# GpSimd makes the lower part of every second block of U, and U's two parts get three buffers each

## The chip, the cores and the metric

The kernel runs on one core of one Trainium2 chip. The metric is the device time of one execution in microseconds (us); lower is better. The engines that matter here are TensorE (PE, with its weight loads as PEld), VectorE (DVE), ScalarE (ACT), GpSimd (POOL), and SyncE (SP), which only issues transfers.

## The reference

The program is a two-layer network over 256 context tokens and 512 latent tokens of width 1024. Each layer has four token mixers and then a feed-forward part with product keys (PEER). Only the PEER part matters for this change. It is, cut to what is computed:

```
q = (xb @ wq).reshape(T, 8, 2, 128)
s = einsum('thcq,hckq->thck', q, keys)             # 128 keys in each of two halves of a head
sv, si = top_k(s, 16)                              # the 16 best of each half
top_s, top_j = top_k(sv[..., 0, :, None] + sv[..., 1, None, :], 16)   # of the 16 x 16 pairs
eidx = the 16 chosen experts of 128 * 128 for every token and head
gate = softmax(top_s)
act = gelu(einsum('td,thkd->thk', xb, U[eidx]))
out = einsum('thk,thkd->td', gate * act, V[eidx])
```

U and V are tables of 16384 rows of 1024 numbers per layer, all float32.

## The kernel before

**Two ways to the experts.** The last tokens of a layer (256 in layer 0, 128 in layer 1) gather just the rows of U and V that they chose. All other tokens (512 in layer 0, 384 in layer 1) are multiplied with all of U and V, in 128 blocks of 128 experts each, and a sparse array of gates decides what counts.

**A block of U.** `s_part(j, up)` (L1451 to L1463) makes one block. SyncE loads 128 x 1024 numbers into `ur`. `split` (L249 to L251) makes two parts of type float32r for TensorE: ScalarE writes the upper part `uh` (a cast, L250), and VectorE writes the lower part `ul = ur - uh` (L251). Then 24 matmuls (L254: eight slices of the width times three products of parts) sum in PSUM under the name `d.S`, ScalarE applies the gelu (`d.pa`, L247) and its queue stores the result to DRAM (`mrg.Ad`, L1472). `uh` and `ul` have two buffers each, so block j + 2 can be cast only when TensorE is done with block j. There are 128 blocks per layer, so 256 casts, 256 subtractions and 6144 matmuls.

**What stands beside it.** `s_ahead(n)` (L1468) lays out the next n blocks of U between pieces of the routing: the scores `rt.q` and `rt.k`, the searches for the best (L1556 to L1583), and `build`, which makes the gate array from one-hot rows (`rt.o`, `rt.og`, `ro.x` on VectorE, `rt.k` on TensorE, `rt.gst` on ScalarE). In layer 1 the last 62 blocks come after all routing (`trailing`).

**The gathers.** `choose(n, after)` (L1511) first uses the rows that came in two calls earlier (`use`: a multiply with sum, L1500, or an addition scaled by a weight, L244, both on VectorE), then copies the numbers of the next rows to `at` (L1522, VectorE) and has GpSimd issue one indirect DMA for each (L1527, into `grow`, of which there are 4 buffers in layer 0 and 6 in layer 1). In layer 0 each block of U carries a call for 2 rows; in layer 1 each of the last 62 blocks carries a call for 1. With `tc.issue_after` the VectorE instructions of a call stand behind the instruction `last[0]`, which is the subtraction of the block just laid out. GpSimd has no other work in these stretches.

**Order.** A scheduler orders each engine's instructions when the program is built, by its own estimate of the times. On the chip each engine runs its list strictly in that order.

After U come the 128 blocks of V (`rt.O`, `d.O`), then the next layer.

Of the kernel before, what the change touches and what calls it, by code (L numbers as in the profile page):

```python
# [13 lines left out]
A = mybir.AluOpType  # L14
# [6 lines left out]
EPS = 1e-6  # L21
# [5 lines left out]
# ---------------------------------------------------------------- layout on the host  # L27
# [90 lines left out]
def consts():  # L118
    o = {}
    for n, L in (("l", SEQ), ("c", CTX)):  # L120
        # Half of the times and of the frequencies: e and o below are the sums and differences of the tokens t and
        # their mirror images, of which the even and the odd frequencies need one each for cosine and sine.
        # 0: the filters, t against L - t; 1, 2: tokens, t + 1/2 against L - t - 1/2, and back.
# [91 lines left out]
# ---------------------------------------------------------------- the program  # L215

def body(tc, I, out, dbg=None, stop=None):
# [56 lines left out]
    def segs(n):  # L274
        """columns in PSUM banks: the latents' 512, then the context's 256 before them"""
        return [(max(0, n - 512), n)] + ([(0, n - 512)] if n > 512 else [])

    with pool("keep") as kp, pool("scr", space=DRAM) as dp:
        # ---------------------------------------------------------- persistent
# [13 lines left out]
        def inv_sqrt(o, i, scale, eps_ap_or_val):  # L293
            """(i * scale + eps) ** -0.5"""
            act(o, i, AF.Ln, scale, eps_ap_or_val)
            act(o, o, AF.Exp, -0.5)
# [10 lines left out]
        # ---------------------------------------------------------- modulation vectors  # L307
        def ada(l, rounds, wp, pp, cs, dma, bufs):
            """columns 2048 * r on; the two vectors' products lie on partitions 32 * q and 32 * q + 1"""
# [23 lines left out]
        # ---------------------------------------------------------- Hyena's filters  # L333
        def dft_part(p, n, L, kind, f):
            """two parts each of the cosines and sines of 128 frequencies"""
            t = T(p, [128, 2, 2, L // 2], F32R, "dft", 2)
            G.dma_start(t, I["dft_" + n][:, kind, f])
            if kind < 2:
                t = t.rearrange("p a b (j m) -> p a b j m", m=128)
            return (t[:, 0, 0], t[:, 0, 1]), (t[:, 1, 0], t[:, 1, 1])  # L340

        def sin_(p, t, ps, frq, bias, L):
            """sin(frq * (ps + bias)) with the argument brought to [-pi, pi]"""
# [13 lines left out]
        def spectrum(l, n, L, p, pp, dst_):  # L357
# [12 lines left out]
            # the first half of the times on the upper partitions; the second, mirrored and with the middle in the  # L370
            # place of time L, on the lower ones
# [10 lines left out]
            # forward plus and minus backward, each the sum (0) and difference (1) of a time and its mirror image  # L382
# [34 lines left out]
            # 1 / (L * (sum of the absolute values + EPS)); 1/L = 2/N is the weight of a frequency in the inverse  # L417
# [5 lines left out]
            for f in range(NC):  # L423
# [15 lines left out]
                if f == 0:  # L439
                    # the highest frequency, in the place of the sine of frequency 0  # L440
# [16 lines left out]
        # ---------------------------------------------------------- prologue  # L457
# [18 lines left out]
        # ---------------------------------------------------------- shared pieces  # L476
        def rms_scale(p, pp, srcs, n, tag, tags=(("sq", 2), ("rstd", 1))):
            """1 / sqrt(mean of squares over all rows + EPS), on every partition"""
# [14 lines left out]
        def norm_mod(hps, p, pp, x, l, which, t0, tag, cut=None):  # L493
            """what the products read, in two parts; for the tokens before and from cut on in a pool each"""
# [16 lines left out]
        def projector(wp, pp, src, tag, off=0, ks=range(8), eng=None):  # L511
            """rows of a product with h for the tokens from t0 on, by segments; early(c) fetches a row's weights"""
# [26 lines left out]
        def padded(p, zd, c, tag, bufs, t0):  # L539
            """a row block of z with two zeros before and one behind each stream, in three stretches of 256 tokens"""  # L540
# [12 lines left out]
        def conv(o, xp, taps, bias, t0):  # L553
            """o = sum of w * (token + shift) + bias; the first tap carries the bias"""
# [26 lines left out]
        # ---------------------------------------------------------- RG-LRU  # L581
# [68 lines left out]
        # ---------------------------------------------------------- RWKV-7  # L650
# [5 lines left out]
        def rwkv_prep(l, zd, t0, pp, p):  # L656
            """what the recurrences read, for both tiles of channels; the long parts go through DRAM"""
# [25 lines left out]
            for c in range(2):  # L683
# [6 lines left out]
                # -- decays, keys and the like, channels on partitions  # L690
# [72 lines left out]
                # -- the masked products N whose (1 - N)^-1 each chunk needs; the inverses of their diagonal blocks  # L763
                # of 16, row by row, with a block on each partition
# [27 lines left out]
                # the gate g: what the read-out multiplies by and adds  # L792
# [26 lines left out]
        def rwkv_load(l, st, p):  # L819
            """what all chunks read"""  # L820
# [15 lines left out]
        def rwkv_chain(l, c, t0, stt_, y, p, pp, qp):  # L836
            """the chunks of 128 tokens of one tile of channels, both directions side by side, as generators that can be
            laid out alternately: the inverses of a chunk, and its recurrence"""
# [10 lines left out]
            def inverse(step):  # L849
# [7 lines left out]
                # Wm[d, s]: C against A and R, B against A and R, with the tokens' order as a mask  # L857
# [11 lines left out]
                # XZ[g, d]: the inverse of direction d where g != d, its transpose where g == d  # L869
# [91 lines left out]
        def rwkv_out(l, t0, n, stt_, y, p, pp, tag):  # L961
            """the read-out of the chunks n of both tiles, normed as a group"""
# [34 lines left out]
        def alternate(*gens):  # L997
            """lays the generators' pieces out in turn; (n, g) begins n rounds later"""
# [6 lines left out]
        # ---------------------------------------------------------- mLSTM  # L1005
        def colmajor(ap, t0):
            """the latents' columns of a token row, walked (row, col) where they lie (col, row)"""
# [185 lines left out]
        # ---------------------------------------------------------- Hyena  # L1193
        def mix_hyena(l, n, zd, ydst, p, pp):
# [16 lines left out]
            for o in range(2):  # L1211
                # sums (0) and differences (1) of the tokens and their mirror images
# [13 lines left out]
                for f in range(NC):  # L1226
# [9 lines left out]
                    # the sine part of the transform is -q[:, 1]  # L1236
# [12 lines left out]
                # what the tokens and their mirror images have in common (0), and half their difference (1)  # L1249
# [22 lines left out]
        # ---------------------------------------------------------- the four mixers  # L1272
# [6 lines left out]
        def mixers(l, xin):  # L1279
            """xin: (pool, tile) of the residual stream"""  # L1280
# [134 lines left out]
        # ---------------------------------------------------------- PEER  # L1415
        def peer(l, xin):
# [5 lines left out]
            # the last tokens gather the rows that they chose; the others' products go over all rows  # L1422
# [21 lines left out]
            # x waits in DRAM while the routing uses its place  # L1444
# [6 lines left out]
            def s_part(j, up):  # L1451
                ur = T(up, [128, 8, 128], F32, "ur", URB[l])
                SP.dma_start(ur, I["U"][l, j])
                uh = T(up, [128, 8, 128], F32R, "uh", 2)
                ul = T(up, [128, 8, 128], F32R, "ul", 2)
                last[0] = split(ur, uh, ul)
# [10 lines left out]
            def s_ahead(n):  # L1467
                """U's products, which don't wait for the routing"""  # L1468
# [9 lines left out]
            def token_rows(t):  # L1478
                """h of a tile of tokens, a token on each partition"""
# [12 lines left out]
            # the last tokens' experts, tile by tile: row e of U, later of V for every token; what has come is used at  # L1492
            # the next calls
# [39 lines left out]
            # ---- routing  # L1533
# [7 lines left out]
            def scores(hc, piece):  # L1541
                """the 16 best keys of half a head for the tokens of a piece"""
# [302 lines left out]
```

## Time and profile before

| | us |
|---|---|
| median of 3 runs | 4990.23 |
| the runs | 4994.22, 4990.23, 4975.98 |
| span of the profiled execution, first to last instruction (no other time of it is given) | 5021.4 |
| its stretch with blocks of U in layer 0 | about 1000 to 2055 |
| its stretch with blocks of U in layer 1 | about 3610 to 4440 |
| blocks of V in layer 0, in layer 1 | about 2090 to 2810, 4440 to 5000 |

The page gives busy times over the whole span, and they mix stages with different limits. What counts here is read from the two stretches with blocks of U: by stretch the busy time of each engine and the granted TensorE clock (1.00 is the level of 2.4 GHz, 0.50 the level of 1.2 GHz), then what TensorE waited for there. Times of instructions overlap on one engine: a matmul of 512 columns shows 0.39 us, but the next begins 0.23 us after it.

### The profile page before, as it was taken

To read this page: it belongs to the slowest core of one execution; us is meant where nothing else is said; L and a number is where in the kernel's file an instruction comes from. 1 tells how busy PE (TensorE), PEld (TensorE's weight loads), DVE (VectorE), ACT (ScalarE), POOL (GpSimd) and SP (SyncE) were. 2 spreads that over 40 slices of the span, in tenths; PEclk is the share of its full clock that TensorE was granted. 3 is DMA by queue.
4 is the path that set the end of the run, shared out by engine and by line. 5 is a ranking of instruction groups with operands and counts; after the bars stand their busy time and mean duration, and the time that the engine had idled before them with its cause. 6 is when DMAs were issued, how large, how long until landed. Compare 5 with 4: busy or idle time off the path is not lost. (4 is left out here: it accounts for less than half of the span.)

```text
span 5021.4 us, 66832 instructions
## 1 busy us (share of the span) xinstructions
PE 4590.8 (91%) x24203; PEld 3842.1 (77%) x24203; DVE 3624.9 (72%) x7303; ACT 1777.9 (35%) x2546; POOL 1375.8 (27%) x1117
## 2 busy tenths in 40 slices
PE   7879898799899999799999887898899998999998
PEld 3658567688777888687788665787688898999997
DVE  5772647399788897688889677556589875567777
ACT  4352222353233444322222335212534443333333
POOL 1211111002344454234455222000002332323332
PEclk9889999899999999899999898968999999999999
DMA  4442545346688999899999544203426889888896
GB/s 177 160 137 77 189 161 158 143 130 236 225 298 307 322 329 332 311 352 353 362 379 381 178 152 134 68 19 110 140 80 231 269 284 345 286 283 325 321 328 248
DMA packets 521083, 1170.01 MB, mean 233 GB/s; under 512 B 68192, under 2 KB 250272, under 8 KB 516272
## 3 DMA queue, kind: packets, MB, share of 16 engines
q1 hardware_dynamic: 227440, 563.42, 32.5%
q0 software_dynamic: 134912, 484.06, 27.2%
q10 hardware_dynamic: 158400, 118.25, 7.3%
q8 instruction: 191, 3.13, 0.3%
q14 instruction: 140, 1.15, 0.1%
HBM read 992.95 MB, written 173.02 MB: 232 GB/s over the span
## 5 line engine op out<-in xcount | busy, mean ns | idle before, releaser
L254 PE MATMUL d.S<-mrg.hhi,d.ul 128*128 128x512 f32 (+1 forms) x2048 | 772.6, 377 | 85.4 <-DVE d.ul L251 76.2
L1527 POOL DMA_INDIRECT d.grow<-in_V_dram,d.at x369 | 578.7, 1568 | 712.2 <-DVE d.at L1522 562.4
L254 PE MATMUL d.S<-mrg.hlo,d.uh 128*128 128x512 f32 (+1 forms) x2048 | 760.2, 371 | 0.1
L254 PE MATMUL d.S<-mrg.hhi,d.uh 128*128 128x512 f32 (+1 forms) x2048 | 757.6, 370 | 0.0
L254 PE MATMUL rt.O<-rt.pv,rt.pv 128*128 128x512 f32 (+1 forms) x2580 | 558.6, 366 | 41.5 <-DVE rt.pv L251 41.0
L254 PEld LDWEIGHTS rt.O<-rt.pv,rt.pv 128*128 128x128 f32 x2580 | 468.3, 189 | 108.8 <-issue 48.9
L254 PEld LDWEIGHTS d.S<-mrg.hhi,d.ul 128*128 128x128 f32 x2048 | 398.1, 194 | 144.5 <-DVE d.ul L251 94.7
L247 ACT ACTIVATE d.pa<-d.S 128x512 f32<-128x512 f32 (+1 forms) x256 | 139.7, 546 | 859.3 <-PE d.S L254 794.3
L254 PEld LDWEIGHTS d.S<-mrg.hlo,d.uh 128*128 128x128 f32 x2048 | 397.8, 194 | 39.2 <-DVE mrg.hlo L251 1.2
L254 PEld LDWEIGHTS d.S<-mrg.hhi,d.uh 128*128 128x128 f32 x2048 | 396.1, 193 | 41.4
L1527 POOL DMA_INDIRECT d.grow<-in_Ur_dram,d.at x233 | 302.9, 1300 | 433.2 <-DVE d.at L1522 326.8
L251 DVE TENSOR_TENSOR d.ul<-d.ur,d.uh 128x1024 fp32r<-128x1024 f32 x256 | 311.6, 1219 | 131.0 <-ACT d.uh L250 130.6
L1527 POOL DMA_INDIRECT rt.grow<-in_Ur_dram,rt.at x151 | 228.8, 1515 | 630.1 <-DVE rt.at L1522 569.4
L250 ACT CAST rt.pv<-rt.vr 128x1024 fp32r<-128x1024 f32 x172 | 181.1, 1053 | 588.0 <-DMA rt.vr<-in_V_dram 249.0
L1500 DVE SCALAR_TENSOR_TENSOR d.grow<-d.grow,rt.tok 128x1024 f32<-128x1024 f32 x233 | 281.9, 1221 | 121.6 <-DMA d.grow<-in_Ur_dram,d.at 120.8
L244 DVE SCALAR_TENSOR_TENSOR d.tok<-d.grow,rt.gw,d.tok 128x1024 f32<-128x1024 f32 x245 | 313.7, 1281 | 51.8 <-DMA d.grow<-in_V_dram,d.at 51.5
L254 PE MATMUL d.O<-rt.pv,rt.pv 128*128 128x512 f32 (+1 forms) x1548 | 337.5, 362 | 0.0
L254 PEld LDWEIGHTS d.O<-rt.pv,rt.pv 128*128 128x128 f32 x1548 | 280.7, 188 | 30.2
L254 PE MATMUL rt.O<-d.pv,d.pv 128*128 128x512 f32 (+1 forms) x1260 | 273.1, 365 | 8.1 <-DVE d.pv L251 7.2
L250 ACT CAST d.uh<-d.ur 128x1024 fp32r<-128x1024 f32 x256 | 267.5, 1046 | 27.7 <-issue 11.5
L254 PEld LDWEIGHTS rt.O<-d.pv,d.pv 128*128 128x128 f32 x1260 | 226.8, 188 | 44.1 <-issue 13.6
L254 PE MATMUL z.z<-hhi,z.wlo 128*128 128x512 f32 (+1 forms) x656 | 236.1, 360 | 23.5 <-POOL z.wlo L251 16.3
(619 smaller groups left out, 9380.0 us busy)
## 6 DMA issues: line engine op xcount, KB each, us to landing
d.ur<-in_U_dram SPq DMA_DIRECT2D x256, 512.0 KB, 5.2
rt.vr<-in_V_dram SPq DMA_DIRECT2D x256, 512.0 KB, 6.0
ada.adaw<-in_ada_w_dram POOLq DMA_DIRECT2D x80, 512.0 KB, 4.1
mrg.Ad<-d.pa ACTq DMA_DIRECT2D x128, 256.0 KB, 5.5
rt.gt<-mrg.Gd SPq DMA_DIRECT2D x32, 1024.0 KB, 9.4
rt.ga<-mrg.Ad SPq DMA_DIRECT2D x128, 256.0 KB, 6.9
mrg.Gd<-ro.x ACTq DMA_DIRECT2D x14, 2048.0 KB, 12.1
mrg.Gd<-rt.gst ACTq DMA_DIRECT2D x14, 2048.0 KB, 14.4
```

Source lines behind the costliest of these rows:

```text
L244: return V.scalar_tensor_tensor(o, a, s, b, op0=op0, op1=op1)
L247: return S.activation(o, i, f, bias=bias, scale=scale)
L250: S.copy(hi, src)
L251: return (eng or V).tensor_tensor(lo, src, hi.bitcast(F32), op=A.subtract)
L254: PE.matmul(ps, l, r, start=start, stop=stop)
L1500: V.scalar_tensor_tensor(g, g, 1.0, s["h"], A.mult, A.mult, accum_out=w[:, e:e + 1])
L1527: G.indirect_dma_start(out=g, out_offset=None, in_=I["Ur"] if r % 256 < 128 else I["V"].rearrange("l j i d -> (l j i) d"), in_offset=bass. ...
```

## The change

All other lines of the diff take out comments and blank them, so that line numbers from here on are 3 higher.

```diff
             def s_part(j, up):
                 ur = T(up, [128, 8, 128], F32, "ur", URB[l])
                 SP.dma_start(ur, I["U"][l, j])
-                uh = T(up, [128, 8, 128], F32R, "uh", 2)
-                ul = T(up, [128, 8, 128], F32R, "ul", 2)
-                last[0] = split(ur, uh, ul)
+                uh = T(up, [128, 8, 128], F32R, "uh", 3)
+                ul = T(up, [128, 8, 128], F32R, "ul", 3)
+                if j % 2:
+                    split(ur, uh, ul, G)
+                else:
+                    last[0] = split(ur, uh, ul)
```

So 64 subtractions per layer move from VectorE's list to GpSimd's, `uh` and `ul` get a third buffer (8 KB more per partition), and the call of `choose` behind an odd block now stands behind the subtraction of the even block before it. What the scheduler makes of this is shown at three places.

GpSimd's list in layer 0, while the gates of the second tile are built; `d.ul` is the lower part of a block of U, `d.grow` and `rt.grow` are gathered rows, `d.at` and `rt.at` the copied row numbers. Before:

```order
L1527 DMA d.grow_12054<-in_Ur_dram,d.at_12052 128x1024
L1527 DMA d.grow_12056<-in_Ur_dram,d.at_12052 128x1024
L1527 DMA d.grow_12096<-in_Ur_dram,d.at_12094 128x1024
L1527 DMA d.grow_12098<-in_Ur_dram,d.at_12094 128x1024
L1527 DMA d.grow_12138<-in_Ur_dram,d.at_12136 128x1024
```

Now:

```order
L1530 DMA d.grow_12054<-in_Ur_dram,d.at_12052 128x1024
L1530 DMA d.grow_12056<-in_Ur_dram,d.at_12052 128x1024
L1530 DMA d.grow_12096<-in_Ur_dram,d.at_12094 128x1024
L1530 DMA d.grow_12098<-in_Ur_dram,d.at_12094 128x1024
L1530 DMA d.grow_12138<-in_Ur_dram,d.at_12136 128x1024
L1530 DMA d.grow_12140<-in_Ur_dram,d.at_12136 128x1024
L251 TENSOR_TENSOR d.ul_12103<-d.ur_12100,d.uh_12102 128x1024
L1530 DMA d.grow_12180<-in_Ur_dram,d.at_12178 128x1024
L1530 DMA d.grow_12182<-in_Ur_dram,d.at_12178 128x1024
```

The list was gathers alone; now the lower part of every second block stands between them, here behind the gathers of three calls, and further gathers stand behind it.

VectorE's list in layer 1, among the last 62 blocks. Before:

```order
L251 TENSOR_TENSOR d.ul_33395<-d.ur_33392,d.uh_33394 128x1024
L1500 SCALAR_TENSOR_TENSOR rt.grow_33351,rt.gw_28715<-rt.grow_33351,rt.tok_28207 128x1024
L1522 COPY rt.at_33427<-rt.ei_28713 128x1
L251 TENSOR_TENSOR d.ul_33434<-d.ur_33431,d.uh_33433 128x1024
L1500 SCALAR_TENSOR_TENSOR rt.grow_33390,rt.gw_28715<-rt.grow_33390,rt.tok_28207 128x1024
L1522 COPY rt.at_33466<-rt.ei_28713 128x1
L251 TENSOR_TENSOR d.ul_33473<-d.ur_33470,d.uh_33472 128x1024
```

Now:

```order
L251 TENSOR_TENSOR d.ul_33395<-d.ur_33392,d.uh_33394 128x1024
L1503 SCALAR_TENSOR_TENSOR rt.grow_33351,rt.gw_28715<-rt.grow_33351,rt.tok_28207 128x1024
L1525 COPY rt.at_33427<-rt.ei_28713 128x1
L1503 SCALAR_TENSOR_TENSOR rt.grow_33390,rt.gw_28715<-rt.grow_33390,rt.tok_28207 128x1024
L1525 COPY rt.at_33466<-rt.ei_28713 128x1
L251 TENSOR_TENSOR d.ul_33473<-d.ur_33470,d.uh_33472 128x1024
```

Every second subtraction is gone, and two calls follow each other without one between them.

TensorE's list at the norm that opens the PEER part of layer 0; `mrg.S` is the last sum of the norm, `rt.q` the first scores. Before:

```order
L254 MATMUL mrg.S_7185<-mrg.sq_7214,cst_60 128x256
L254 MATMUL d.S_7351<-mrg.hhi_7222,d.ul_7347 128x512
L254 MATMUL rt.q_7301<-mrg.hhi_7224,rt.wlo_7172 128x256
L254 MATMUL rt.q_7301<-mrg.hlo_7225,rt.whi_7171 128x256
L254 MATMUL rt.q_7301<-mrg.hhi_7224,rt.whi_7171 128x256
L254 MATMUL d.S_7351<-mrg.hlo_7223,d.uh_7346 128x512
L254 MATMUL d.S_7351<-mrg.hhi_7222,d.uh_7346 128x512
```

Now:

```order
L254 MATMUL mrg.S_7185<-mrg.sq_7214,cst_60 128x256
L254 MATMUL rt.q_7301<-mrg.hhi_7224,rt.wlo_7172 128x256
L254 MATMUL rt.q_7301<-mrg.hlo_7225,rt.whi_7171 128x256
L254 MATMUL rt.q_7301<-mrg.hhi_7224,rt.whi_7171 128x256
L254 MATMUL rt.q_7301<-mrg.hhi_7224,rt.wlo_7172 128x256
L254 MATMUL rt.q_7301<-mrg.hlo_7225,rt.whi_7171 128x256
```

The first block of U (24 matmuls) and 13 matmuls of the second stood between the first scores; now the first block begins when two and a half rounds of scores are done.

## Rows read from the trace of the kernel before

**Rows 1.** The page's head and busy times over the whole span, one row kept.
```profile
span 5021.4 us, 66832 instructions
...
PE 4590.8 (91%) x24203; PEld 3842.1 (77%) x24203; DVE 3624.9 (72%) x7303; ACT 1777.9 (35%) x2546; POOL 1375.8 (27%) x1117
```

**Rows 2.** Busy us of PE, PEld, DVE, ACT, POOL by stretch; clock, DMA, GB/s.
```profile
1100.00:1480.00 380.00, 352.34 (x1594) 287.13 (x1593) 332.61 (x1110) 116.17 (x166) 121.32 (x97) 0.96 0.70 240
1480.00:2010.00 530.00, 514.37 (x2600) 428.21 (x2599) 458.21 (x714) 221.71 (x262) 251.34 (x164) 0.99 0.94 322
3750.00:4180.00 430.00, 388.52 (x2319) 376.98 (x2317) 347.89 (x672) 197.19 (x241) 116.59 (x76) 0.92 0.79 266
4180.00:4440.00 260.00, 249.38 (x1404) 246.13 (x1405) 150.26 (x240) 87.99 (x124) 84.90 (x58) 0.98 0.87 298
```

**Rows 3.** TensorE's waits in these stretches, in their order: us, times, longest.
```profile
PE d.S L254 <- DVE d.ul L251: 25.2, 6, 10.9
...
PE d.S L254 <- DVE d.ul L251: 14.9, 11, 3.3
...
PE d.S L254 <- DVE d.ul L251: 24.9, 10, 6.1
...
PE d.S L254 <- DVE d.ul L251: 11.2, 7, 6.6
```

**Rows 4.** Timeline of TensorE around the longest wait: start, us; idle time in brackets.
```profile
1339.54 0.39 PE L254 MATMUL d.S<-mrg.hlo,d.uh 128*128 128x512 f32 x1
1339.77 0.39 PE L254 MATMUL d.S<-mrg.hhi,d.uh 128*128 128x512 f32 x1
1351.03 0.79 PE L254 MATMUL d.S<-mrg.hhi,d.ul 128*128 128x512 f32 x1 [10.87 <-DVE d.ul L251]
...
1355.03 0.63 PE L254 MATMUL d.S<-mrg.hhi,d.ul 128*128 128x512 f32 x1
1355.46 0.63 PE L254 MATMUL d.S<-mrg.hlo,d.uh 128*128 128x512 f32 x1
```

**Rows 5.** Timeline of ScalarE and VectorE at that wait.
```profile
1340.69 1.04 ACT L250 CAST d.uh<-d.ur 128x1024 fp32r<-128x1024 f32 x1
...
1341.31 1.22 DVE L1500 SCALAR_TENSOR_TENSOR d.grow<-d.grow,rt.tok 128x1024 f32<-128x1024 f32 x1 [6.95 <-DMA d.grow<-in_Ur_dram,d.at]
...
1349.76 1.22 DVE L251 TENSOR_TENSOR d.ul<-d.ur,d.uh 128x1024 fp32r<-128x1024 f32 x1
```

**Rows 6.** Granted clock in the 5 us after that wait, columns as in rows 2.
```profile
1351.00:1356.00 5.00, 4.97 (x12) 3.91 (x13) 2.93 (x13) 0.00 (x0) 3.64 (x4) 0.50 0.92 303
```

**Rows 7.** Subtraction on VectorE (mean ns, 1480:2010), on GpSimd elsewhere (min/median/max ns).
```profile
L251 DVE TENSOR_TENSOR d.ul<-d.ur,d.uh 128x1024 fp32r<-128x1024 f32 x76 | 92.5, 1217 | 29.1 <-ACT d.uh L250 29.0
...
L251 POOL TENSOR_TENSOR wlo<-wraw,whi x4: 2334/2348/2472, 55.5 to 2817.7; 128x1024 fp32r<-128x1024 f32 x4
```

**Rows 8.** Timeline of VectorE and GpSimd where the subtraction runs on GpSimd.
```profile
54.48 0.96 DVE L236 TENSOR_TENSOR nt<-x,rstd 128x768 f32<-128x768 f32 x1 [0.98 <-ACT rstd L247]
...
55.53 3.09 DVE L236 TENSOR_TENSOR nt<-x,rstd 128x768 f32<-128x768 f32 x1
...
55.47 2.33 POOL L251 TENSOR_TENSOR wlo<-wraw,whi 128x1024 fp32r<-128x1024 f32 x1 [50.78 <-ACT whi L250]
```

**Rows 9.** Timeline of GpSimd and VectorE in layer 0 at the longest gather.
```profile
1820.51 9.09 POOL L1527 DMA_INDIRECT d.grow<-in_V_dram,d.at  x1 [0.65 <-DVE d.tok L244]
1830.33 0.94 POOL L1527 DMA_INDIRECT d.grow<-in_V_dram,d.at  x1 [0.73 <-DVE d.at L1522]
...
1820.16 2.35 DVE L236 TENSOR_TENSOR rt.og<-rt.o,rt.ijT 128x2048 f16<-128x2048 f16 x2
```

**Rows 10.** VectorE by line, largest groups of 1480 to 2010 and 1100 to 1480.
```profile
L244 DVE SCALAR_TENSOR_TENSOR d.tok<-d.grow,rt.gw,d.tok 128x1024 f32<-128x1024 f32 x118 | 150.9, 1279 | 21.8 <-DMA d.grow<-in_V_dram,d.at 21.8
...
L1500 DVE SCALAR_TENSOR_TENSOR d.grow<-d.grow,rt.tok 128x1024 f32<-128x1024 f32 x76 | 91.6, 1220 | 41.6 <-DMA d.grow<-in_Ur_dram,d.at 41.3
L251 DVE TENSOR_TENSOR d.ul<-d.ur,d.uh 128x1024 fp32r<-128x1024 f32 x43 | 52.2, 1215 | 2.1 <-ACT d.uh L250 2.1
```

## The prediction, made before the changed kernel ran

> **What bounds the kernel now.** The page comes first: TensorE is busy for 91% of the span [rows 1], so it is the engine to be freed, and time can be won only where it stands still or runs slowly. The second view is the busy time by stretch, because the change touches only the blocks of U. In the four stretches with nearly all of them TensorE is busy for 352 of 380, 514 of 530, 389 of 430 and 249 of 260 us; VectorE comes next with 333, 458, 348 and 150 [rows 2], which is 88%, 86%, 81% and 58%. GpSimd is far from full (121, 251, 117 and 85 us). The third view is what ended TensorE's waits: the lower part `ul` of a block came late 34 times, for 25.2 + 14.9 + 24.9 + 11.2 = 76.2 us [rows 3]. That sum is the pool from which the change can draw.
>
> The fourth view is the timeline of the longest of these waits. TensorE ended a block at 1340.2 and got the next `ul` 10.87 us later [rows 4]. ScalarE's cast of that block was done at 1341.7, but VectorE had just waited 6.95 us for a gathered row, did that row and a search first, and came to `ul` only at 1349.76 [rows 5]. So the delay is one of place in VectorE's list, and of two buffers, which let the cast begin only when a block is finished. The wait had a second price: for 5 us behind it the granted clock was 0.50, the lower level [rows 6], and matmuls followed each other at 0.43 us instead of 0.23 [rows 4]. Twelve matmuls at 0.43 instead of 0.23 are 2.4 us.
>
> **The change part by part.** Sums are made against the profiled span of 5021.4 us, which is 0.6% above the median of the runs; the difference is then taken from the median.
>
> *The third buffer.* A block's cast and subtraction may begin one block earlier: 24 matmuls at 0.23 us are 5.5 us in layer 0. Of the longest waits of the four stretches (10.9, 3.3, 6.1 and 6.6 us) only the first is much over that [rows 3], so nearly all could go, if the lists let it. It will not always, since a `ul` on VectorE still stands behind gathered rows, and one on GpSimd behind gathers. Ends: nothing, and 76. I take two thirds, 51 us, as half of the blocks leave VectorE's list and the rest gain a lead that is longer than most waits.
>
> *The clock behind these waits.* The mean wait is 76.2 / 34 = 2.2 us. I reckon that a dozen of the 34 are long enough to be followed by a slow piece like that of rows 6; 12 x 2.4 is 29 us, two thirds of that 20. Ends: 0 and 29.
>
> *The subtraction on GpSimd.* One on VectorE takes 1.22 us; on GpSimd 2.35 us (median of four) [rows 7]. TensorE does not see that length as such, with one block of lead more. What it sees is VectorE being held. While GpSimd did such a subtraction from 55.47 to 57.80, a VectorE product of two tiles that takes 0.96 us took 3.09, and was done 0.8 us after GpSimd [rows 8]. In the other direction a gather on GpSimd that takes 0.94 us alone took 9.09 while VectorE ran products of two tiles back to back [rows 9]. The two engines take turns, whole instructions at a time. The Trainium skill says the same (SBUF — State Buffer, section "Who interferes with whom"): an instruction of VectorE with two inputs in SBUF and one of GpSimd that reads SBUF exclude each other, and the second "fully blocks". Rows 8 agree; in rows 9 GpSimd lost not one instruction but a run of them.
>
> VectorE's work in these stretches is nearly all of that kind: row products, one-hot products, subtractions [rows 9, 10]. So each moved subtraction gives VectorE 1.22 us and takes up to 2.35: from -1.22 (VectorE was idle anyway) to +1.13. Half of the 43 and 76 blocks of layer 0's stretches [rows 7, 10] are 21 and 38. At +1.13 they bring VectorE from 333 to 356 of 380 us (94%) and from 458 to 501 of 530 (95%). In layer 1, with its 64 moved blocks put half into each stretch, it comes to 384 of 430 (89%) and 186 of 260 (72%). In layer 0 a list that already loses 41 us to late rows in the first stretch and 22 in the second [rows 10] cannot hide all of this; I take half of 24 + 43 us as time, 33 us, and nothing in layer 1. Ends: 0 (all of it falls into idle time) and 67 + 36.
>
> *GpSimd's queue.* A `ul` stands behind up to three calls' gathers, and gathers stand behind it. It can be late by what the gathers wait for, which is VectorE's copy of row numbers. Before, GpSimd stood empty for over half of each stretch [rows 2], so its own 2.4 us per two blocks (530 us for 76 blocks are 14 us for two) have room. A gather is then used two calls later, as before. I price this at nothing by itself; the cover is the two buffers ahead, and if it is gone the case is rival 2.
>
> *The calls behind odd blocks* now follow the even block's subtraction directly. The same row products, copies and gathers are made, up to one block earlier. No cost.
>
> *The norm of layer 0.* Some 37 matmuls of U stood between the first scores while the norm was still being made; they now come later, when TensorE is full: 37 x 0.23 = 8.5 us. In turn two casts and two subtractions (2 x 1.22 us on VectorE) leave the norm's own path, 2.4 us. Together +6. Transfers stay the same in number and size: SyncE still loads a block per `ur` buffer, of which there are as many as before.
>
> **Sum:** -51 - 20 + 33 + 6 = -32 us, so 4990 - 32 = **4958 us**. A measurement of this kernel tells about 0.5% (25 us) from no change.
>
> **Rivals.**
>
> 1. *VectorE becomes the bound in layer 0: slower.* Place: 1100 to 2010. If GpSimd's turns nearly always meet VectorE at work, the full 67 us stretch those two, TensorE waits for VectorE there and loses 10 us more to the lower clock (four pieces of 2.4), the norm adds 6, and only layer 1 gains: two thirds of its 36 us of waits, and half of the 20 us of clock. 67 + 10 + 6 - 24 - 10 = +49, so 5039 us. It decides from the point where VectorE's demand with its waits for rows passes the stretch: 501 + 22 of 530 us in the second stretch is just under it. For it speaks that nearly all of VectorE's work there has two inputs; against it that VectorE has 47 and 72 us idle in these stretches, 41 and 22 of them in waits for rows, which are open to GpSimd's turns. The skill's page named above would make this the rule wherever both engines are busy, and its page Perfetto Trace Analysis (Optimizing Scalar/DVE Operations) warns that moving work between these two "might not help"; no row here shows the two this busy together.
>
> 2. *The waits change their name: no change.* The `ul` on GpSimd comes late for the same reason as before, since the gathers ahead of it wait for copies that VectorE makes after a late row. Then half the gain stays: -25 - 10 + 33 + 6 = +4, 4994 us. For it: the new list of GpSimd. Against it: the third buffer gives both lists a lead of one block.
>
> 3. *The whole pool is drawn: faster by more.* -76 - 29 + 6 = -99, 4891 us, if GpSimd's turns fall into VectorE's idle time. For it: in layer 1 VectorE has 82 and 110 us idle. Against it: layer 0.
>
> **How the numbers follow.** The forecast gets 0.43, with a range of its own from 4930 to 4985; rival 1 gets 0.20, rival 2 0.20, rival 3 0.17. The unknown price of a turn (-1.22 to +1.13 per block) is what separates them. For 8 in 10 the range runs from 4905, with half of rival 3 inside, to 5040, with rival 1's time inside. Faster by over 0.5% (under 4965): two thirds of the forecast and all of rival 3, 0.45. Slower by over 0.5% (over 5015): rival 1 and a little of rival 2, 0.22. The rest, 0.33, is no change.
>
> **What would show it.** Right: waits of TensorE for `ul` (of VectorE and GpSimd together) of 25 to 30 us instead of 76; clocks of the first and third stretch above 0.96 and 0.92; subtractions on GpSimd of 2.4 to 4 us; VectorE's two-input instructions with means above those of rows 10, at 93 to 96% busy in layer 0. Wrong: VectorE's row products and one-hot products with means of 1.5 us and more and new waits of TensorE for `rt.og` in layer 0 (rival 1); `ul` waits of the same sum, released by GpSimd (rival 2); unchanged VectorE means with hardly a wait left (rival 3). If the order of U's blocks against the routing shifted the start of V, that would be a step I have not priced.

## The result, and the profile after

The changed kernel takes 5056.42 us (median of 9 runs), the kernel before 4989.68 us beside it (9 runs): a ratio of 1.013, with a 95% interval from 1.0089 to 1.0171. The change makes the kernel slower by 1.3%, some 65 us, and the time lies above the forecast range (4905 to 5040). The profiled execution has a span of 5074.9 us. Most executions of all kernels here fall into two groups some 45 us apart, and in the traces this difference lies in the mixers of layer 1 (mostly about 740 or 785 us from the last product of V to the norm before the next PEER part), so single traces are compared stretch by stretch.

The page after, its head and busy times (before: [rows 1]):

```profile
span 5074.9 us, 66938 instructions
...
PE 4582.9 (90%) x24203; PEld 3843.5 (76%) x24203; DVE 3613.9 (71%) x7175; ACT 1777.7 (35%) x2546; POOL 1693.2 (33%) x1245
```

The four stretches with blocks of U after, columns as in [rows 2]; those of layer 1 begin 50 us later than before:

```profile
1100.00:1480.00 380.00, 349.04 (x1595) 285.11 (x1595) 328.46 (x1151) 111.03 (x166) 161.88 (x112) 0.96 0.66 226
1480.00:2010.00 530.00, 479.95 (x2434) 403.53 (x2434) 424.45 (x628) 213.51 (x253) 305.20 (x188) 0.95 0.90 302
3800.00:4230.00 430.00, 369.38 (x2304) 359.78 (x2302) 357.24 (x650) 195.72 (x240) 222.33 (x108) 0.93 0.78 263
4230.00:4490.00 260.00, 251.25 (x1416) 249.97 (x1417) 132.65 (x213) 87.87 (x123) 142.95 (x88) 0.98 0.88 303
```

In the second stretch TensorE is busy for 480 us where it was 514 (2434 matmuls instead of 2600), at a clock of 0.95 instead of 0.99, and VectorE for 424 instead of 458. TensorE does less although VectorE has become emptier. What TensorE waits for in the four stretches (before: [rows 3]):

```profile
PE d.S L254 <- POOL d.ul L251: 21.6, 4, 12.9
PE d.S L254 <- DVE d.ul L251: 8.2, 3, 6.9
...
PE rt.k L254 <- ACT ro.x L247: 19.2, 5, 4.3
PE rt.k L254 <- ACT rt.gst L247: 17.0, 4, 5.5
PE d.S L254 <- DVE d.ul L251: 9.5, 4, 5.2
PE d.S L254 <- POOL d.ul L251: 5.4, 3, 3.2
...
PE rt.k L254 <- ACT rt.gst L247: 20.3, 5, 6.1
PE rt.k L254 <- ACT ro.x L247: 12.0, 3, 4.8
PE d.S L254 <- POOL d.ul L251: 10.8, 4, 3.7
PE d.S L254 <- DVE d.ul L251: 9.2, 7, 4.0
...
PE d.S L254 <- POOL d.ul L251: 15.7, 5, 7.7
```

The waits for `ul` are 80.4 us where they were 76.2, and 53.5 of them now name GpSimd. New beside them are waits of the gate products `rt.k` for ScalarE, which empties their PSUM tiles: 68.5 us, of which 16.0 were there before (15.8 of them in layer 1).

VectorE in 1480 to 2010 by line (before: [rows 10] and [rows 7]), and the subtraction on both engines over the whole run (min/median/max ns):

```profile
L244 DVE SCALAR_TENSOR_TENSOR d.tok<-d.grow,rt.gw,d.tok 128x1024 f32<-128x1024 f32 x103 | 142.9, 1388 | 50.0 <-DMA d.grow<-in_V_dram,d.at 49.5
L251 DVE TENSOR_TENSOR d.ul<-d.ur,d.uh 128x1024 fp32r<-128x1024 f32 x35 | 44.2, 1263 | 25.5 <-ACT d.uh L250 17.2 <-PE d.S L254 8.3
```

```profile
L251 DVE TENSOR_TENSOR d.ul<-d.ur,d.uh x128: 1171/1220/4021, 1035.3 to 4475.0; 128x1024 fp32r<-128x1024 f32 x128
L251 POOL TENSOR_TENSOR d.ul<-d.ur,d.uh x128: 2342/2414/4917, 1037.5 to 4480.9; 128x1024 fp32r<-128x1024 f32 x128
```

How the two engines hold each other shows in the timeline around GpSimd's longest subtraction of layer 0, GpSimd first, then VectorE:

```profile
1541.25 4.92 POOL L251 TENSOR_TENSOR d.ul<-d.ur,d.uh 128x1024 fp32r<-128x1024 f32 x1 [4.47 <-ACT d.uh L250]
...
1541.57 1.21 DVE L251 TENSOR_TENSOR d.ul<-d.ur,d.uh 128x1024 fp32r<-128x1024 f32 x1
1542.70 1.21 DVE L1503 SCALAR_TENSOR_TENSOR d.grow<-d.grow,rt.tok 128x1024 f32<-128x1024 f32 x1
1543.85 0.08 DVE L1503 DVE_READ_ACCUMULATOR d.grow<-d.grow,rt.tok 128x1 f32 x1
1543.85 3.40 DVE L1503 SCALAR_TENSOR_TENSOR d.grow<-d.grow,rt.tok 128x1024 f32<-128x1024 f32 x1
```

VectorE's two instructions from 1541.57 run in their usual 1.21 us, and GpSimd stands meanwhile; then GpSimd does its 2.4 us until 1546.17, and VectorE's next product is done 1.08 us after that. Each of the 12 row products over 2.5 us in 1100 to 2010 ended 1.08 to 1.09 us after a subtraction of GpSimd. In layer 0 the means of VectorE's two-input products rise with this: 1388 ns against 1279 in the first row above.

Summed over the trace, each VectorE instruction that ran beside a subtraction of GpSimd and took at least 0.3 us more than the median of its kind (same line, tiles and shape): 41 in layer 0 with 70.4 us of excess, 35 in layer 1 with 63.6. That is 134 us for 128 subtractions, 1.05 us each, where each had freed 1.22 us. Such an excess is called a hold here.

### The profile page after: what moved, and what is told of

Its sections match the earlier page's. It is cut to its first block, busy times and chain, and to the rows that moved or that the text cites. A ratio compares the mean times of both kernels' runs of the same rounds, so it can differ in the third digit from the quotient of the medians.

```text
span 5074.9 us, 66938 instructions
## 1 busy us (share of the span) xinstructions
PE 4582.9 (90%) x24203; PEld 3843.5 (76%) x24203; DVE 3613.9 (71%) x7175; ACT 1777.7 (35%) x2546; POOL 1693.2 (33%) x1245
## 5 line engine op out<-in xcount | busy, mean ns | idle before, releaser
L1530 POOL DMA_INDIRECT d.grow<-in_V_dram,d.at x369 | 559.0, 1515 | 658.9 <-DVE d.at L1525 532.4
L251 POOL TENSOR_TENSOR d.ul<-d.ur,d.uh 128x1024 fp32r<-128x1024 f32 x128 | 334.6, 2614 | 546.1 <-ACT d.uh L250 493.6
L1503 DVE SCALAR_TENSOR_TENSOR d.grow<-d.grow,rt.tok 128x1024 f32<-128x1024 f32 x233 | 301.1, 1302 | 133.8 <-DMA d.grow<-in_Ur_dram,d.at 133.1
L244 DVE SCALAR_TENSOR_TENSOR d.tok<-d.grow,rt.gw,d.tok 128x1024 f32<-128x1024 f32 x245 | 327.1, 1335 | 82.7 <-DMA d.grow<-in_V_dram,d.at 81.5
L254 PE MATMUL rt.k<-rt.og,ro.x 128*128 128x128 f16 x1792 | 221.3, 297 | 77.9 <-ACT rt.gst L247 41.6
L251 DVE TENSOR_TENSOR d.ul<-d.ur,d.uh 128x1024 fp32r<-128x1024 f32 x128 | 175.2, 1370 | 155.2 <-ACT d.uh L250 146.8
```

Source lines behind the costliest of these rows:

```text
L244: return V.scalar_tensor_tensor(o, a, s, b, op0=op0, op1=op1)
L251: return (eng or V).tensor_tensor(lo, src, hi.bitcast(F32), op=A.subtract)
L254: PE.matmul(ps, l, r, start=start, stop=stop)
L1503: V.scalar_tensor_tensor(g, g, 1.0, s["h"], A.mult, A.mult, accum_out=w[:, e:e + 1])
L1530: G.indirect_dma_start(out=g, out_offset=None, in_=I["Ur"] if r % 256 < 128 else I["V"].rearrange("l j i d -> (l j i) d"), in_offset=bass. ...
```

## The experiments

First theory, from the new waits: **A**, the third buffer changes TensorE's list (in the changed kernel the gate products stand in unbroken groups of 24 and 40, before they were partly spread), so that TensorE waits for ScalarE. Rivals: **B**, `ul` late on GpSimd and too few `ur` buffers; **C**, VectorE held by GpSimd's subtractions. Ratios are to the kernel before, run beside each. The edits are cut to the lines that matter. e4, e6, e7, e9 and e14 also give a small tile, `te`, one buffer instead of two to make room; e9 shows no cost of that.

### One half of the change at a time

e1, the third buffer alone (from before; `ul` likewise):

```diff
-                uh = T(up, [128, 8, 128], F32R, "uh", 2)
+                uh = T(up, [128, 8, 128], F32R, "uh", 3)
```

> The third buffer alone: uh and ul have three buffers, every subtraction stays on VectorE. Theory A (with the third buffer the order puts the gate products rt.k into unbroken groups of 24 to 128 matmuls, and TensorE waits for ScalarE to empty their three PSUM tiles): the change's loss is here too, 1.008 to 1.015 of the kernel before, with 35 to 45 us of waits of TensorE's rt.k for ScalarE in layer 0's U blocks (0.2 us before). Theory B (a ul on GpSimd comes late behind gathers, and ur's two buffers take back the lead) and theory C (GpSimd's subtractions hold VectorE): no loss without GpSimd, 0.990 to 1.000.

Measured: 4992.26 us, ratio 1.0013 (0.9975 to 1.0052).

e2, GpSimd alone (from the changed kernel; `ul` likewise):

```diff
-                uh = T(up, [128, 8, 128], F32R, "uh", 3)
+                uh = T(up, [128, 8, 128], F32R, "uh", 2)
```

> GpSimd alone: every second ul on GpSimd, uh and ul with two buffers as before; in this order rt.k is spread as before. Theory A: rt.k waits below 5 us in layer 0, 0.990 to 1.003 of the kernel before. Theory B: ul comes late behind gathers without the third buffer more than with it, 1.010 or more. Theory C: VectorE is held as in the changed kernel, 1.010 to 1.015, with the product of gathered rows on VectorE at 1.30 us as there.

Measured: 5112.34 us, ratio 1.0274 (1.0235 to 1.0313). Theory A falls: the loss comes with GpSimd. e2's time lies above what C expected (1.010 to 1.015) and fits B, so B is left to e4 and e12. The third buffer alone gains nothing either, and makes good half of what GpSimd costs. TensorE's waits in e1 from 1100 to 2010:

```profile
PE d.S L254 <- DVE d.ul L251: 17.5, 7, 4.5
PE rt.k L254 <- ACT rt.gst L247: 7.3, 3, 4.4
PE rt.k L254 <- ACT rt.q L1545: 5.1, 2, 2.6
...
PE rt.k L254 <- ACT ro.x L247: 4.3, 3, 2.5
```

Of 40.1 us for `ul` [rows 3] 17.5 are left, as hoped, but 16.7 us for ScalarE have come in their place.

### Removing the two waits that the trace names

e3, five PSUM tiles for the gate products (from the changed kernel; `k` has four buffers everywhere):

```diff
-                                pg = T(psQ, [128, 4, 128], F32, "k", 3)
+                                pg = T(psQ, [128, 4, 128], F32, *(("q", 1) if (t16 // 4 + t4) % 5 == 4 else ("k", 4)))
```

> The changed kernel, with the gate products going round five PSUM tiles instead of three. Theory A: the waits of rt.k for ScalarE in layer 0 (42 us in the changed kernel) fall below 12 us, and the time to 0.995 to 1.003 of the kernel before. Theories B and C: waits for ul and VectorE's means stay, 1.010 to 1.015.

e4, a third `ur` (from the changed kernel):

```diff
-URB = (2, 3)
+URB = (3, 3)
```

> The changed kernel with a third ur buffer in layer 0 (te with one buffer to make room); rt.k stands in groups as in the changed kernel. Theory B: the casts of ScalarE no longer wait 190 us for ur, waits for ul in layer 0 halve (43 to some 20 us), 1.000 to 1.005 of the kernel before. Theory A: at most 10 us better than the changed kernel, 1.010 to 1.015. Theory C: as the changed kernel, 1.010 to 1.015.

Measured: e3 5069.0 us, 1.0173 (1.0122 to 1.0224); e4 5058.85 us, 1.0157 (1.0102 to 1.0213). Neither helps. In e3 28.9 us of these waits stay from 1100 to 2010, where the changed kernel has 36.2. In e4's trace the waits for ScalarE are gone, and most of their time is now spent at `ul`: 67.0 us in 1100 to 2010, where the changed kernel has 44.7 us for `ul` and 36.2 for ScalarE.

```profile
PE d.S L254 <- POOL d.ul L251: 36.7, 12, 11.7
PE d.S L254 <- DVE d.ul L251: 30.3, 7, 10.9
```

So the waits of `rt.k` look like a sign of a loss that lies further back (e3 took only a fifth of them away), and a shortage of `ur` buffers is not the cause.

### Which part of GpSimd's work costs

All from e1. Theory **D** is new: GpSimd's list stops at a subtraction that waits for its cast, and the gathers behind it are late. **E**: the `ul` of GpSimd itself is late.

e5, a tiny subtraction that waits like the moved one:

```diff
                 last[0] = split(ur, uh, ul)
+                if j % 2:
+                    ux = T(up, [128, 2], F32R, "ux", 1)
+                    G.tensor_tensor(ux, ur[:, 0, 0:2], uh[:, 0, 0:2].bitcast(F32), op=A.subtract)
```

> e1 (three buffers, every subtraction on VectorE), and behind each odd block's cast a subtraction of 128 x 2 numbers on GpSimd whose result nobody reads: it waits for the cast and holds ur and uh as the moved subtraction does, but hardly takes GpSimd's time or VectorE's turn. Theory A has fallen. Theory D (GpSimd's list now stops at a subtraction that waits for its cast, the gathers behind it start late, VectorE waits for their rows): the changed kernel's loss is mostly here, 1.008 to 1.015 of the kernel before, with over 110 us of VectorE's waits for rows in layer 0's U blocks (74 in e1, 132 in the changed kernel). Theory C (VectorE held by GpSimd's subtraction) and theory E (the ul of GpSimd itself comes late to TensorE): as e1, 1.000 to 1.004.

e6, the whole subtraction a second time:

```diff
+                if j % 2:
+                    ux = T(up, [128, 8, 128], F32R, "ux", 1)
+                    G.tensor_tensor(ux, ur, uh.bitcast(F32), op=A.subtract)
```

> e1, and GpSimd does the whole subtraction of each odd block a second time, into a tile that nobody reads (te with one buffer to make room): GpSimd's list and its turns against VectorE are those of the changed kernel, but VectorE is not relieved and TensorE waits for VectorE's ul alone. Theory D: 1.008 to 1.018. Theory C: more than the changed kernel, 1.015 to 1.030, as VectorE keeps 1.22 us per block and loses its turns too. Theory E: 1.000 to 1.004.

e7, the same work without waits, on a tile of zeros, 114 times (`lg` is the last gather laid out; later gathers stand behind `dry`):

```diff
+                if j % 2 and lg[0] is not None:
+                    with tc.issue_after(lg[0].ins):
+                        dry[0] = G.tensor_tensor(ux, ux.bitcast(F32), ux.bitcast(F32), op=A.subtract)
```

> e1, and 101 subtractions of 128 x 1024 numbers on GpSimd between the gathers, of a tile of zeros with itself: they wait for no cast, and only take GpSimd's time and VectorE's turns (te with one buffer to make room). Theory C: 101 instead of 128 of them, 1.008 to 1.015. Theories D and E: 1.000 to 1.005.

Measured: e5 1.0018 (0.999 to 1.0047), e6 1.0222 (1.0178 to 1.0265), e7 1.0103 (1.0066 to 1.0141). D falls with e5. e6 and e7 make no `ul` late on GpSimd and lose all the same, so E does not explain them; C stands. e6, in which VectorE keeps its subtractions, loses more than the changed kernel (1.0222 against 1.013), so beside the holds the relief of VectorE is worth something.

e9 and e14, e7 with another instruction in the same place:

```diff
-                        dry[0] = G.tensor_tensor(ux, ux.bitcast(F32), ux.bitcast(F32), op=A.subtract)
+                        G.memset(ux.bitcast(F32), 0.0)
+                        dry[0] = G.memset(ux.bitcast(F32), 0.0)
```

```diff
-                        dry[0] = G.tensor_tensor(ux, ux.bitcast(F32), ux.bitcast(F32), op=A.subtract)
+                        dry[0] = G.tensor_copy(ux, ux.bitcast(F32))
```

> e7 with each of its subtractions replaced by two memsets of the same tile on GpSimd (0.95 us each in e7's trace, so 1.9 us, as the shortest of e7's subtractions): the same time of GpSimd between the gathers, but nothing is read. Theory C (a GpSimd instruction that reads two tiles holds VectorE): 1.000 to 1.004 of the kernel before, and VectorE's product of gathered rows back at 1.22 us (1.35 in e7). Theory G (GpSimd's time alone makes the gathers late): 1.007 to 1.012, as e7.

> e7 with a copy of the tile of zeros onto itself in the place of the subtraction: GpSimd reads one tile instead of two. If any reading by GpSimd holds VectorE, VectorE's product of gathered rows stays near 1.35 us and the time at 1.005 to 1.012 (a copy is at most as long as e7's 1.9 us); if only two-tile instructions of both exclude each other, 1.22 us and 0.997 to 1.003.

Measured: e9 0.9959 (0.992 to 0.9998), e14 1.0041 (0.9998 to 1.0083). GpSimd's instruction (min/median/max ns), and under it VectorE's product of gathered rows from 1100 to 2100, in e7, e14 and e9:

```profile
L1459 POOL TENSOR_TENSOR mrg.ux<-mrg.ux x114: 1893/1912/3572, 1140.2 to 4474.7; 128x1024 fp32r<-128x1024 f32 x114
...
L1506 DVE SCALAR_TENSOR_TENSOR d.grow<-d.grow,rt.tok 128x1024 f32<-128x1024 f32 x116 | 155.9, 1357 | 54.9 <-DMA d.grow<-in_Ur_dram,d.at 54.5
```

```profile
L1459 POOL CAST mrg.ux<-mrg.ux x114: 1042/1059/2732, 1132.7 to 4403.2; 128x1024 fp32r<-128x1024 f32 x114
...
L1506 DVE SCALAR_TENSOR_TENSOR d.grow<-d.grow,rt.tok 128x1024 f32<-128x1024 f32 x121 | 159.2, 1328 | 61.6 <-DMA d.grow<-in_Ur_dram,d.at 61.5
```

```profile
L1459 POOL MEMSET mrg.ux<- x114: 954/971/1032, 1122.6 to 4349.5; 128x1024 f32 x114
...
L1507 DVE SCALAR_TENSOR_TENSOR d.grow<-d.grow,rt.tok 128x1024 f32<-128x1024 f32 x124 | 150.0, 1221 | 62.3 <-DMA d.grow<-in_Ur_dram,d.at 62.1
```

Two memsets take GpSimd as long as one subtraction, are never drawn out beyond 1.12 us, leave VectorE's product at its 1.22 us, and cost no time. (That e9 stands a little below e1 does not come from the stretches with blocks of U, which are 1106.8 and 814.7 us long in its trace and 1108.4 and 808.3 in e1's; where it comes from is not shown.) For VectorE's two-input products it is GpSimd's reading that holds: by the runs 114 times 1.9 us of reading cost 1.0%, and 114 times 1.06 us some 0.4%, with an interval that reaches none; in the traces layer 0 (norm to V, table below) is 52 and 23 us longer than in e1. e14's time lies between the two that were expected; reading one tile holds as well, and less. GpSimd's time as such costs nothing here. The Trainium skill has this rule (SBUF — State Buffer, section "Who interferes with whom"): a VectorE instruction with two inputs in SBUF contends with a GpSimd instruction that reads SBUF, "not with one that only writes it". e7, e14 and e9 agree. The memsets are not without holds either: in e9's trace 44 small instructions of VectorE, mostly copies and operations with a scalar, took 28.6 us too long beside them (up to 1.28 us each), but none of its row products or subtractions, and no time was lost by it.

e15, the changed kernel with the subtraction in quarters:

```diff
-                    split(ur, uh, ul, G)
+                    S.copy(uh, ur)
+                    for k in range(0, 8, 2):
+                        G.tensor_tensor(ul[:, k:k + 2], ur[:, k:k + 2], uh[:, k:k + 2].bitcast(F32), op=A.subtract)
```

> The changed kernel with GpSimd's subtraction in four pieces of 128 x 256, two slices each. If VectorE is held for one whole instruction of GpSimd at a time, a hold is at most 0.7 us instead of up to 2.8, and the mean product of gathered rows falls from 1.36 us towards 1.25: 1.003 to 1.010. If the pieces follow each other without giving the turn away, as in the changed kernel: 1.010 to 1.016.

Measured: 5073.99 us, 1.0212 (1.0144 to 1.0281): no better, and rather worse, though its interval overlaps that of the changed kernel. Single holds are shorter (0.55 us instead of 1.76 on average), but there are almost three times as many (214 with 117 us, by the sum used above), and GpSimd needs 566 us for its 512 pieces where it needed 335 for 128 wholes. In the traces the loss is in layer 0 (norm to V 1194.3 us, the changed kernel 1156.9); layer 1 is shorter (824.8 against 839.5).

### What VectorE's freed time is worth

e10, only the place of the calls (from e1):

```diff
-                last[0] = split(ur, uh, ul)
+                ins = split(ur, uh, ul)
+                if j % 2 == 0:
+                    last[0] = ins
```

> e1, with the calls behind odd blocks standing behind the even block's subtraction, as in the changed kernel; nothing on GpSimd but gathers. Theory F (two calls that follow each other make the rows late): 1.005 to 1.010 of the kernel before, with over 110 us of VectorE's waits for rows in layer 0's U blocks (74 in e1). Theories C and G: 0.999 to 1.004.

e11 leaves the odd blocks' subtraction out, and with `last[0]` set at even blocks alone it has e10's place of the calls too (from e1):

```diff
-                last[0] = split(ur, uh, ul)
+                if j % 2:
+                    S.copy(uh, ur)
+                    ul = uh
+                else:
+                    last[0] = split(ur, uh, ul)
```

e12 has GpSimd do it for nobody (from e11):

```diff
-                    S.copy(uh, ur)
+                    ux = T(up, [128, 8, 128], F32R, "ul", 3)
+                    split(ur, uh, ux, G)
                     ul = uh
```

> The odd blocks' subtraction is left out, on GpSimd and on VectorE: the products of odd blocks read uh in the place of ul. It shows what the change would be worth if GpSimd's work cost nothing and were never late. Theory C: VectorE's freed 1.22 us per odd block are worth something, 0.988 to 0.997 of the kernel before. Theory H (VectorE's time was never worth anything with three buffers): 0.998 to 1.003.

> e11, with the odd blocks' subtraction done on GpSimd into a tile that no product reads: GpSimd and VectorE have the work of the changed kernel, but TensorE never waits for GpSimd. Theory C: the loss is in VectorE's holding, so this is within 0.004 of the changed kernel, 1.009 to 1.016. Theory E (the ul of GpSimd comes late to TensorE): 1.000 to 1.004 or what e11 gives.

Measured: e10 1.0038 (0.9999 to 1.0076), e11 1.0002 (0.9963 to 1.0042), e12 1.0134 (1.0075 to 1.0193). e11 is as fast as the kernel before, but its partner is e10: against it, relief of VectorE alone gains 0.0036, 18 us, which is within the intervals, and in the traces 27 us in layer 0 (1096.6 against 1123.9) and nothing in layer 1. In e12, where no product waits for GpSimd's `ul`, the whole loss of the change is back: 1.3% above e11. So B and E are not needed for it by the runs. Whether the place of the calls costs a little (e10), the interval leaves open; in the traces e10 is 15 us longer than e1 in layer 0 and 13 in layer 1.

### By layer, and a better version

e8, e1 with five PSUM tiles (the edit of e3):

> e1 with the gate products going round five PSUM tiles instead of three. e1's trace has 14 us (layer 0) and 30 us (layer 1) of waits of rt.k for ScalarE: if TensorE sees them as time, a half to all of them go, 0.992 to 0.997 of the kernel before; if they only take the place of waits for ul, as e3 suggests, 0.999 to 1.003.

e13 and e17 (the same kernel twice), three buffers in layer 1 alone, every subtraction on VectorE (from before; `ul` likewise):

```diff
-                uh = T(up, [128, 8, 128], F32R, "uh", 2)
+                uh = T(up, [128, 8, 128], F32R, "uh", 2 + l)
```

e16, the same with GpSimd in layer 1:

```diff
+                if l and j % 2:
+                    split(ur, uh, ul, G)
+                else:
+                    last[0] = split(ur, uh, ul)
```

> Every subtraction on VectorE, two buffers in layer 0 and three in layer 1. If the third buffer gains in layer 1 (e1's trace: 31 us less from the norm to the first block of V than before) and layer 0 gives it back, 0.993 to 0.997 of the kernel before; if it is worth nothing in either layer, 0.998 to 1.003.

> The whole change in layer 1 alone: three buffers and every second subtraction on GpSimd there, layer 0 as before. If the holding costs nothing in layer 1, as the prediction had it, the time is that of e17. If it costs there what the single traces say (some 20 us), 0.003 to 0.006 more than e17, and about that of the kernel before, 0.997 to 1.002.

> The kernel of e13 again, as the partner of e16: three buffers in layer 1, every subtraction on VectorE. If e13's gain is real, 0.991 to 0.998 of the kernel before.

Measured: e8 0.9996 (0.9967 to 1.0026), so five tiles win nothing without GpSimd either; e13 0.9918 (0.9863 to 0.9973); e17 0.9972 (0.9929 to 1.0015); e16 1.0035 (1.0 to 1.0071). By the means of all 12 runs both e13 (4953.9 against 4972.8) and e17 (4965.8 against 4985.9) stand at 0.996, so 0.9918 is taken as too low. This version is then some 0.4% faster than the kernel before and, by the ratios, 1.7% than the changed one, the first of the two at the edge of what can be measured. Beside e17 GpSimd costs 0.0063 in layer 1, 31 us, by the runs; in the two traces the stretch of layer 1 differs by 17 us (831.2 against 814.1).

## Why the prediction was wrong

The stretch from a layer's norm before PEER (its first sum on TensorE) to the first product of V, in us, and in layer 0 VectorE's instructions without overlap and its idle time:

| kernel | layer 0 | VectorE busy, idle there | layer 1 |
|---|---|---|---|
| before | 1101.8 | 920, 182 | 839.1 |
| e1, third buffer | 1108.4 | 918, 190 | 808.3 |
| e17, third buffer in layer 1 | 1093.7 | 920, 173 | 814.1 |
| e16, e17 with GpSimd in layer 1 | 1090.1 | 921, 169 | 831.2 |
| e9, memsets on GpSimd | 1106.8 | 925, 182 | 814.7 |
| e10, e1 with the calls' new place | 1123.9 | 918, 206 | 821.1 |
| e11, odd subtractions left out | 1096.6 | 850, 247 | 826.3 |
| e12, e11 with GpSimd at work | 1152.0 | 927, 225 | 822.5 |
| e14, copies on GpSimd | 1131.6 | 961, 171 | 810.6 |
| e7, without waits on GpSimd | 1160.7 | 996, 165 | 820.4 |
| changed kernel | 1156.9 | 920, 237 | 839.5 |

These are single traces. Through layer 0 TensorE, VectorE, ScalarE and GpSimd run the same lists in e13, e16 and e17 as in the kernel before, and the stretches took 1093.9, 1090.1 and 1093.7 us there, where the trace of before took 1101.8; so a difference of some 10 us says nothing. The trace of the kernel before is also a long one (5021.4 us against a median of 4990), and it is the only one with two buffers in layer 1 and no work on GpSimd, so its 839.1 us may be too much.

**The third buffer and the clock behind its waits: the step that failed most.** They were to bring 51 + 20 = 71 us; e1 measured +6 us (1.0013; from -12 to +26). The step took two thirds of the waits for `ul` as time. In layer 1 something of it came true: 31 us less in e1's trace, 25 in e17's, and some 0.4% (20 us) in the runs of e13 and e17. In layer 0 the waits for `ul` did fall, from 40.1 to 17.5 us, but the same buffer changes TensorE's list: the gate products stand together and wait 16.7 us for ScalarE, and U begins later (its first product 41 us after the norm's first sum instead of 18). The stretch is 7 us longer than in the trace of the kernel before and 15 to 18 us longer than in the other three traces of that list; the prediction had 6 of this as the norm's term. That the new list makes these waits is how its rows and e1's waits read; an order of before with three buffers was not run.

**The subtraction on GpSimd: the right mechanism in layer 0, too small a sum.** Predicted +33 us, in layer 0 alone; measured from 1.0013 to 1.013, that is +58 us, which takes in the calls' new place. The price of a turn was well placed: 1.05 us of holding against 1.22 freed, so -0.2 us per block, inside the -1.22 to +1.13 given. What failed is netting the two. In the table VectorE is as busy after as before, 920 us. But of e11's freed 68 us (beside e10) 41 became idle time, mostly waits for gathered rows, and only 27 came off the stretch; the holds of e7 and e12 (78 and 77 us more busy time than e1 and e11) made it 52 and 55 us longer. The reading is that freed time fell in large part where VectorE waited for rows anyway, while held time falls on a list that runs in order, and TensorE, ScalarE and the next `ur` wait behind it.

Step by step (the scheduler reorders VectorE's list a little at each), the traces of layer 0 go from before to the changed kernel as follows: +7 us for the third buffer, +15 for the calls' new place, -27 for the subtractions left out, +55 for GpSimd doing them, +5 for products that read GpSimd's `ul`. In layer 1 the same steps are -31, +13, +5, -4 and +17. So in layer 0 GpSimd's reading beside VectorE explains the loss, as the memsets of e9 take the same time of GpSimd and cost nothing. "Nothing in layer 1" was wrong too, by 17 us in the traces of e16 and e17 and 31 us in their runs, but there the cause stays open: e12 has 89 us of holds in layer 1 and no longer stretch than e11, and the changed kernel loses its 17 us where products read GpSimd's `ul`, for which TensorE waits 26.5 us there.

**Two figures of the prediction were too low.** 64 moved blocks at +1.13 us are 72 us in layer 1, where its upper end has 36. And the 22 us of waits for rows in the second stretch are those of one line alone, L244; with the other lines, of which the largest follows here from the trace before, they come to 42 us, so that by rival 1's own measure (501 + 42 of 530 us) VectorE was past its point and not just under it:

```profile
L1500 DVE SCALAR_TENSOR_TENSOR d.grow<-d.grow,rt.tok 128x1024 f32<-128x1024 f32 x33 | 39.8, 1221 | 10.9 <-DMA d.grow<-in_Ur_dram,d.at 10.6
```

Of the forecast's own signs two failed: waits for `ul` of 25 to 30 us (80.4 were measured), and VectorE at 93 to 96% busy in layer 0 (86% and 80%).

**Rival 1** came nearest in time (5039) and had the holds as its mechanism, but VectorE did not become the bound, and its signs came only in part: the large groups of VectorE's products have means of 1.27 to 1.53 us in the second stretch, where 1.5 and more were named, and there are no waits for `rt.og` in layer 0. **Rival 2** had its sign, the same sum of `ul` waits (80.4 for 76.2), two thirds of it under GpSimd's name; but by the runs e12 has the loss without a single such wait, and rival 2's time (4994) was far too low. In layer 1 its mechanism may have a part, as said above. One wait shows its mechanism well, the longest (12.94 us), in the timelines of ScalarE, GpSimd and TensorE:

```profile
1371.10 1.04 ACT L250 CAST d.uh<-d.ur 128x1024 fp32r<-128x1024 f32 x1 [5.54 <-DMA d.ur<-in_U_dram]
...
1380.28 1.34 POOL L1530 DMA_INDIRECT d.grow<-in_Ur_dram,d.at  x1 [0.30 <-issue]
1381.64 2.35 POOL L251 TENSOR_TENSOR d.ul<-d.ur,d.uh 128x1024 fp32r<-128x1024 f32 x1
...
1384.05 0.80 PE L254 MATMUL d.S<-mrg.hhi,d.ul 128*128 128x512 f32 x1 [12.94 <-POOL d.ul L251]
```

The cast was done at 1372.14, and the subtraction began 9.5 us later, behind gathers.

**What held.** GpSimd's queue priced at nothing, in layer 0: its list may wait (e5), its time is free (e9), and late `ul` cost 5 us there by the traces. GpSimd's subtraction at 2.4 us. The calls behind odd blocks at no cost is not shown: e10's runs leave up to 0.8% open, and its trace is 15 us longer in layer 0. Clocks of the first and third stretch were 0.96 and 0.93, about the signs named, but the second fell from 0.99 to 0.95, which no term had.

## What to carry to other kernels

Before moving work from VectorE to GpSimd, look at what VectorE does beside it: where that has two inputs in SBUF, a GpSimd instruction that reads gives most of the freed time back as holds (here 1.05 of 1.22 us), and they must not be netted: in layer 0 some 40% of the freed time came off the stretch (27 of 68 us), and some 70% of the held time was added to it (55 of 77). Instructions that only write cost nothing here. And a wait that a bigger buffer removes is no gain until the stretch gets shorter: look at the new order of the list, and give the buffer only to the stage where it does.

## What was not expected of the hardware

Each of the 12 longest row products of VectorE ended 1.08 to 1.09 us after the subtraction of GpSimd that it met. GpSimd stands back too: its subtraction of 2.4 us took up to 4.92 us where VectorE's two-input instructions followed each other. A copy that reads only one tile holds VectorE too (holds up to 1.56 us in e14). And cutting GpSimd's instruction into four did not pay in layer 0: the holds fell from 134 to 117 us over the run, and GpSimd's own time rose from 335 to 566 us.
